# A static ring of five weight tiles, a separate tile of sums in the first FFN parts, and one more seven-product pair in groups 3 and 7

## The chip, the cores and the metric

The kernel runs on one core of one Trainium2 chip. TensorE does the matrix products, ScalarE and VectorE prepare the weights, GpSimd issues some of the DMAs and SyncE issues most of the rest. The metric is the device time of one execution in microseconds; the median of three runs of the kernel before is 2088.28 us (2087.98 to 2088.78).

## The reference

Two pre-norm layers work on a residual stream of 256 tokens by 2048 columns, all in float32. Layer 0 mixes tokens with two groups of heads (windowed attention and a chunked mLSTM), layer 1 with a forgetting attention. After the mixer each layer has the same feed-forward network, and only that is touched here:

```
x = x + mixer(rms_norm(x, g1))
y = rms_norm(x, g2)
x = x + (silu(y @ w_gate) * (y @ w_up)) @ w_down     # w_gate, w_up: 2048 x 5632, w_down: 5632 x 2048
```

A final norm ends it. The weights arrive in float32 and are read once.

## The kernel before

**Precision.** Each weight chunk is 128 partitions by 2 by 512 (256 rows of the matrix by 512 columns, 512 KB). ScalarE casts it to a shorter type (`hi`, a "cast"), VectorE subtracts that from the raw chunk (`lo`), and TensorE forms one product from three matmuls, hi by high part of the activations, lo by high part, hi by low part (`three`, L533 to L535). The function `split_chunk` (L188, L189) does this for a chunk as loaded, `split_plain` (L357, L358) for anything that was computed first. `hi` and `lo` rotate through eight pairs of tiles (`slot`).

**Staging of the feed-forward network.** The 5632 hidden columns are cut into 11 groups of 512 gate and 512 up columns, numbered 0 to 10. They are worked in three parts: groups 0 to 2, 3 to 6 and 7 to 10. Each part is followed by its share of the down-projection (two calls of `pair_group`, four blocks of 512 output columns). `ffn` holds these loops. The activations of a group are joined after its products: VectorE and ScalarE make silu(gate) times up in a tile `c`, four transposing DMAs on SyncE's queue (L709) turn it, and ScalarE and VectorE copy and split it into `mh` and `ml` during the next group. The last group of the first part uses TensorE transposes instead (L693).

**Pairs.** Inside a group (`pair_group`), eight pairs of 256 rows of the inner dimension are worked in the order of a table of (kind, pair). Kind 0, a plain pair, takes the gate chunk and the up chunk as they are: 8 products, 24 matmuls. Kind 1, a mixed pair, combines gate and up chunk before the products in the manner of Winograd and Strassen and takes seven products, 21 matmuls. A mixed pair needs the raw tile `ra` (gate), the raw tile `rb` (up), and the sum and differences of them. `ORDER` has three mixed pairs (1, 3 and 5, each between plain ones); `HEAVY`, used in groups 4, 5, 8 and 9 (`DENSE`), has four, each followed by a plain one.

**Where the sum is made.** In groups 3 to 10 and their down-projections (`adding`) the gate chunk is read a second time by a DMA that GpSimd issues and that adds into half of `rb` (L600). It waits for the load of `rb`, and the cast of `rb` waits for it. In groups 0 to 2 and their down-projection VectorE makes the sum (L606). Then, in both cases: `rb` is split into `hu`, `lu` (a 1024-element cast and subtraction), VectorE makes `rb[:,1]` (L608, 512) and all of `ra` (L610, 1024) from it, and those are split into `hc`, `lc` (512) and `hd`, `ld` (1024).

**What sets the order.** The program is written in one sequence; the framework's scheduler then decides the order of each engine's instructions and places the waits. The raw tiles of mixed pairs come from a pool with five buffers (`RAWS`, tag "raw", `load_raw` L135): a new tile takes the buffer that was given up first. Raw tiles of plain pairs come from another pool of four buffers. Each engine and each DMA queue works strictly in its own order.

## Time and profile before

| what | value |
|---|---|
| median of the runs | 2088.28 us (2087.98 to 2088.78, n = 3) |
| the profiled execution | 2086.12 us, its span 2084.4 us |
| TensorE busy in the span | 2066.4 us (99%) |
| VectorE busy | 1804.5 us (87%) |
| ScalarE busy | 1383.7 us (66%) |
| layer 0: groups 0 to 2 | 322.4 to 453.0 us |
| layer 0: down-projection of the first part | 453.0 to 519.0 us |
| layer 0: groups 3, 4, 5, 6 | from 519.0, 560.5, 601.3, 642.1 to 683.6 us |
| layer 0: groups 7 to 10 | 766.5 to 931.1 us |
| layer 1: groups 0 to 2 and their down-projection | 1385.0 to 1511.2 and to 1579.2 us |
| layer 1: groups 3 to 6, 7 to 10 | 1579.2 to 1743.7, 1826.7 to 1991.3 us |

In a timeline row the columns are start, duration, engine, source line, operation, output<-inputs, shape and count; in brackets stands the idle time before it and what ended that. A row with x6 stands for six instructions of its kind in a row. In a windows row the columns are the stretch, its length, then busy time (count) of TensorE, its weight loads, VectorE, ScalarE and GpSimd, the granted TensorE clock, the share of the DMA engines and GB/s. In a row of the groups, count, busy time and mean duration in ns are followed by the idle time before and what ended it. SPq is SyncE's DMA queue.

### The profile page before, as it was taken

To read this page: it belongs to the slowest core of one execution; us is meant where nothing else is said; L and a number is where in the kernel's file an instruction comes from. 1 tells how busy PE (TensorE), PEld (TensorE's weight loads), DVE (VectorE), ACT (ScalarE), POOL (GpSimd) and SP (SyncE) were. 2 spreads that over 40 slices of the span, in tenths; PEclk is the share of its full clock that TensorE was granted. 3 is DMA by queue.
4 is the path that set the end of the run, shared out by engine and by line. 5 is a ranking of instruction groups with operands and counts; after the bars stand their busy time and mean duration, and the time that the engine had idled before them with its cause. 6 is when DMAs were issued, how large, how long until landed. Compare 5 with 4: busy or idle time off the path is not lost.

```text
span 2084.4 us, 26995 instructions
## 1 busy us (share of the span) xinstructions
PE 2066.4 (99%) x9449; PEld 1713.1 (82%) x9449; DVE 1804.5 (87%) x2235; ACT 1383.7 (66%) x1760; POOL 113.2 (5%) x143
## 2 busy tenths in 40 slices
PE   9999999999999999999999999999999999999998
PEld 7878887887888888888888888888878888888887
DVE  6788768999899998998899688679998999899994
ACT  6777677765567656767677776687655677557763
POOL 1010000000000000000010000000000000000000
PEclk9999999999999999999999999999999999999999
DMA  8566577666778777778676766587657777867864
GB/s 292 175 208 197 189 252 227 187 204 213 210 225 265 232 233 237 226 240 218 205 211 208 229 198 185 155 265 227 222 174 235 236 220 239 259 205 209 265 206 150
DMA packets 320664, 455.07 MB, mean 218 GB/s; under 512 B 107644, under 2 KB 115856, under 8 KB 320400
## 3 DMA queue, kind: packets, MB, share of 16 engines
q1 hardware_dynamic: 307088, 426.27, 64.9%
q0 software_dynamic: 12720, 25.99, 6.8%
q8 instruction: 74, 1.21, 0.2%
q10 hardware_dynamic: 720, 1.09, 0.2%
q14 instruction: 62, 0.51, 0.1%
HBM read 428.87 MB, written 2.12 MB: 207 GB/s over the span
## 4 chain that ended last, share of the span: by engine, by line
PE 86%; DMA 4%; DVE 4%; ACT 4%; issue 3%; SPq 0%; ACTq 0%; POOLq 0%; POOL 0%; DVEq 0%
PE acc L533 19%; PE acc L534 19%; PE acc L535 19%; PE prod L533 5%; PE prod L534 5%; PE prod L535 5%; PE acc L224 4%; PE acc L223 4%; PE acc L225 4%; DVE lo L189 1%; DMA raw<-in_w_down_dram 1%; ACT hi L188 1%; DMA raw<-in_w_gate_dram 1%; PE p L387 1%; ACT box L323 1%
## 5 line engine op out<-in xcount | busy, mean ns | idle before, releaser
L189 DVE TENSOR_TENSOR lo<-raw,hi 128x1024 fp32r<-128x1024 f32 (+3 forms) x648 | 762.7, 1192 | 148.5 <-ACT hi L188 146.2
L188 ACT CAST hi<-raw 128x1024 fp32r<-128x1024 f32 (+3 forms) x648 | 654.0, 1027 | 352.9 <-PE acc L535 130.1
L534 PE MATMUL acc<-lo,xh 128*128 128x512 f32 x1272 | 495.0, 390 | 0.0
L535 PE MATMUL acc<-hi,xl 128*128 128x512 f32 x1272 | 493.9, 390 | 0.0
L533 PE MATMUL acc<-hi,xh 128*128 128x512 f32 x1272 | 480.5, 391 | 2.4 <-ACT hi L188 2.4
L357 ACT CAST hi<-raw 128x1024 fp32r<-128x1024 f32 (+1 forms) x323 | 286.9, 894 | 193.7 <-DVE raw L608 78.2
L358 DVE TENSOR_TENSOR lo<-raw,hi 128x1024 fp32r<-128x1024 f32 (+1 forms) x323 | 328.3, 1026 | 31.2 <-ACT hi L357 30.4
L533 PEld LDWEIGHTS acc<-hi,xh 128*128 128x128 f32 x1272 | 239.4, 188 | 53.6 <-ACT hi L188 4.0
L534 PEld LDWEIGHTS acc<-lo,xh 128*128 128x128 f32 x1272 | 239.6, 188 | 49.7 <-issue 0.2
L535 PEld LDWEIGHTS acc<-hi,xl 128*128 128x128 f32 x1272 | 239.3, 188 | 49.9
L534 PE MATMUL acc<-lo,mh 128*128 128x512 f32 x466 | 181.4, 390 | 0.0
L535 PE MATMUL acc<-hi,ml 128*128 128x512 f32 x466 | 180.8, 389 | 0.0
L533 PE MATMUL acc<-hi,mh 128*128 128x512 f32 x466 | 176.3, 389 | 4.4 <-ACT hi L357 4.4
L610 DVE TENSOR_TENSOR raw<-raw 128x1024 f32<-128x1024 f32 x103 | 125.6, 1220 | 0.9
L224 PE MATMUL acc<-lo,mh 128*128 128x512 f32 (+1 forms) x322 | 126.3, 392 | 0.0
L223 PE MATMUL acc<-hi,mh 128*128 128x512 f32 (+1 forms) x322 | 125.8, 391 | 0.0
L225 PE MATMUL acc<-hi,ml 128*128 128x512 f32 (+1 forms) x322 | 123.7, 391 | 0.0
L533 PEld LDWEIGHTS acc<-hi,mh 128*128 128x128 f32 x466 | 87.5, 188 | 23.0 <-ACT hi L357 4.9
L534 PEld LDWEIGHTS acc<-lo,mh 128*128 128x128 f32 x466 | 87.6, 188 | 18.2
L535 PEld LDWEIGHTS acc<-hi,ml 128*128 128x128 f32 x466 | 87.6, 188 | 18.2
L224 PE MATMUL acc<-lo,xh 128*128 128x512 f32 (+3 forms) x288 | 99.9, 347 | 0.2 <-DVE lo L189 0.2
L225 PE MATMUL acc<-hi,xl 128*128 128x512 f32 (+3 forms) x288 | 98.8, 344 | 0.0
(362 smaller groups left out, 3033.1 us busy)
## 6 DMA issues: line engine op xcount, KB each, us to landing
raw<-in_w_gate_dram SPq DMA_DIRECT2D x176, 512.0 KB, 5.3
raw<-in_w_up_dram SPq DMA_DIRECT2D x176, 512.0 KB, 5.2
raw<-in_w_down_dram SPq DMA_DIRECT2D x176, 512.0 KB, 5.7
raw<-in_w_in_odd_dram SPq DMA_DIRECT2D x88, 512.0 KB, 5.1
raw<-in_w_in_even_dram SPq DMA_DIRECT2D x51, 512.0 KB, 4.7
raw<-in_w_out_even_dram SPq DMA_DIRECT2D x32, 512.0 KB, 5.1
raw<-in_w_out_odd_dram SPq DMA_DIRECT2D x32, 512.0 KB, 4.7
raw<-in_w_gate_dram POOLq DMA_DIRECT2D x56, 256.0 KB, 5.7
```

Of the source, the lines that this page charges most:

```text
L188: latest[0] = nc.scalar.copy(hi[:, k, 0:n], raw[:, k, 0:n])
L189: nc.vector.tensor_tensor(out=lo[:, k, 0:n], in0=raw[:, k, 0:n], in1=hi[:, k, 0:n].bitcast(F32), op=ALU.subtract)
L223: nc.tensor.matmul(o, ah[:, ts], hi, start=(k == 0), stop=False)
L224: nc.tensor.matmul(o, ah[:, ts], lo, start=False, stop=False)
L225: nc.tensor.matmul(o, al[:, ts], hi, start=False, stop=(k == k_all - 1 and cs.stop == n))
L323: nc.scalar.copy(ju[:, :, b], turned[:, b, :, :, :].rearrange("p k t q -> p (k t q)"))
L357: nc.scalar.copy(dst_h, src)
L358: nc.vector.tensor_tensor(out=dst_l, in0=src, in1=dst_h.bitcast(F32), op=ALU.subtract)
L533: nc.tensor.matmul(o, ah, hi, start=start, stop=False)
L534: nc.tensor.matmul(o, ah, lo, start=False, stop=False)
L535: nc.tensor.matmul(o, al, hi, start=False, stop=stop)
L610: nc.vector.tensor_tensor(out=ra, in0=ra, in1=both, op=ALU.subtract)
```

## The change

There are three edits.

1. **Five fixed tiles.** The pool tag with five buffers is replaced by a list `ring` of five tiles, raw0 to raw4, made once per layer. In groups 3 to 10 and their down-projections `load_raw` takes them strictly in turn (ra, rb, ra, rb, ...), so the tile of an `rb` is the one that the `ra` of two mixed pairs earlier had, and the tile of an `ra` is the one that the `rb` of three pairs earlier had.
2. **Groups 0 to 2 and their down-projection.** Only raw0 to raw3 take loads there, and raw4 is a tile of sums, `t4`. The half `rb[:,1]` is split as loaded (512). VectorE then makes `t4[0]` = rb0 + ra0, `t4[1]` = rb1 - rb0, `ra[0]` = t4[0] - rb1, `ra[1]` = ra1 - ra0, four instructions of 512, and splits `t4` and `ra` (1024 each). The same seven products follow.
3. **Groups 3 and 7** use the table `PLAIN_FIRST`: four mixed pairs in the order 0, 1, 2, 3, 5, 4, 7, 6, where 1, 3, 5 and 7 are mixed; 3 and 5 are next to each other. The fourth pair's sums are already there, for `HEAVY`.

```diff
--- before.py
+++ after.py
@@ -35,6 +35,7 @@
 FILL = 16
 ORDER = ((0, 0), (1, 1), (0, 2), (1, 3), (0, 4), (1, 5), (0, 6), (0, 7))
 HEAVY = ((1, 1), (0, 0), (1, 3), (0, 2), (1, 5), (0, 4), (1, 7), (0, 6))
+PLAIN_FIRST = ((0, 0), (1, 1), (0, 2), (1, 3), (1, 5), (0, 4), (1, 7), (0, 6))
 FOURTH = 7
 DENSE = (4, 5, 8, 9)
 ADDING = 3
@@ -53,7 +54,6 @@
 W_RAWS = 4
 LATER = (6, 10, 3, 5)
 LATER_DOWN = (5, 6)
-RAWS = 5
 P_JOIN = 4
 COLD = 9
 TURNED = (0,)
@@ -125,6 +125,7 @@
     xt = gp.tile([P, KT, S], F32, name="xt")
 
     loaded = [None]
+    ring = []
 
     def load_raw(w, k0, c0, n, pool=wr, bufs=4, raws=None):
         if raws:
@@ -349,7 +350,7 @@
         elif n == 3:
             halves = [fp.tile([P, 3, NB], F32, tag=f"sd{i}", name="box", bufs=1)[:, 0:CK, :] for i in range(2)]
         else:
-            halves = [fp.tile([P, CK, NB], F32, tag="raw", name="box", bufs=RAWS) for _ in range(2)]
+            halves = ring[2:4]
         flat, turned = (a.rearrange("p a n -> p (a n)") for a in halves)
         return flat, turned.bitcast(U16).rearrange("p (b k t q) -> p b k t q", b=2, t=NT, q=P)
 
@@ -594,16 +595,14 @@
             first, last = 1 not in kinds[:pos], 1 not in kinds[pos + 1 :]
             if first:
                 prods = [bank(1 - par, "prod") for _ in range(4)]
-            ra, rb = (load_raw(w, k0, c0, NB, fp, W_RAWS if halves else RAWS, raws) for w, c0 in mats)
+            ra, rb = (load_raw(w, k0, c0, NB, fp, W_RAWS, raws) for w, c0 in mats)
             if adding:
                 (w, c0), part = mats[0], slice(k0 * P, (k0 + 1) * P)
                 nc.gpsimd.dma_start(rb[:, 0, :], w[part, c0 : c0 + NB], accum_op=ALU.add)
             hg, lg = split_chunk(ra, NB)
             run_due(todo, pos)
             hu, lu = slot()
-            if halves is None:
-                if not adding:
-                    nc.vector.tensor_tensor(out=rb[:, 0, :], in0=ra[:, 0, :], in1=rb[:, 0, :], op=ALU.add)
+            if adding:
                 split_plain(hu, lu, rb)
                 nc.vector.tensor_tensor(out=rb[:, 1, :], in0=rb[:, 0, :], in1=rb[:, 1, :], op=ALU.subtract)
                 both = rb[:, 1, :].rearrange("p (a n) -> p a n", a=1).broadcast_to([P, CK, NB])
@@ -614,6 +613,20 @@
                 split_plain(hd, ld, ra)
                 ht = [hu[:, 0, :], hd[:, 0, :], hc, hd[:, 1, :]]
                 lt = [lu[:, 0, :], ld[:, 0, :], lc, ld[:, 1, :]]
+            elif halves is None:
+                t4 = ring[4]
+                split_plain(hu[:, 1, :], lu[:, 1, :], rb[:, 1, :])
+                nc.vector.tensor_tensor(out=t4[:, 0, :], in0=rb[:, 0, :], in1=ra[:, 0, :], op=ALU.add)
+                nc.vector.tensor_tensor(out=t4[:, 1, :], in0=rb[:, 1, :], in1=rb[:, 0, :], op=ALU.subtract)
+                nc.vector.tensor_tensor(out=ra[:, 0, :], in0=t4[:, 0, :], in1=rb[:, 1, :], op=ALU.subtract)
+                nc.vector.tensor_tensor(out=ra[:, 1, :], in0=ra[:, 1, :], in1=ra[:, 0, :], op=ALU.subtract)
+                parts = []
+                for src in (t4, ra):
+                    hs, ls = slot()
+                    split_plain(hs, ls, src)
+                    parts.append((hs, ls))
+                ht = [parts[a][0][:, b, :] for a in range(2) for b in range(2)]
+                lt = [parts[a][1][:, b, :] for a in range(2) for b in range(2)]
             else:
                 split_plain(hu[:, 1, :], lu[:, 1, :], rb[:, 1, :])
                 nc.vector.tensor_tensor(out=ra[:, 0, :], in0=rb[:, 0, :], in1=ra[:, 0, :], op=ALU.add)
@@ -645,6 +658,7 @@
 
     def ffn(layer, fp, sx, x4, sd, key, todo, idx_next=None, key_next=None, finish=None):
         r = rstd(key)
+        early_ring = ring[0:4]
 
         def sums_x(pair):
             if pair == FOURTH:
@@ -664,8 +678,9 @@
                     x_of,
                     sums_x,
                     [(w_gate[layer], g * NB), (w_up[layer], g * NB)],
-                    HEAVY if g in DENSE else ORDER,
+                    HEAVY if g in DENSE else PLAIN_FIRST if g in (3, 7) else ORDER,
                     todo,
+                    raws=ring if g0 >= ADDING else early_ring,
                     adding=g0 >= ADDING,
                 )
                 todo = []
@@ -757,7 +772,8 @@
                         close(acc, n)
                     continue
                 plain, c = pair_group(
-                    fp, 1 - n0 // 2, m_of, sums_d, [(wd, n0 * NB), (wd, (n0 + 1) * NB)], order, todo, adding=g0 >= ADDING
+                    fp, 1 - n0 // 2, m_of, sums_d, [(wd, n0 * NB), (wd, (n0 + 1) * NB)], order, todo,
+                    raws=ring if g0 >= ADDING else early_ring, adding=g0 >= ADDING
                 )
                 todo = []
                 if end and idx_next is None:
@@ -777,12 +793,14 @@
             nd = max(len(mixed_of(o)) for o in DOWN.values())
             sx = [fp.tile([P, nx, 4, P], F32R, name=f"sx{i}", bufs=1) for i in range(2)]
             x4 = fp.tile([P, 2, P], F32R, name="x4", bufs=1)
+            ring.extend(fp.tile([P, CK, NB], F32, name=f"raw{i}", bufs=1) for i in range(5))
             todo = out_proj(w_out, idx, key, (*sx, x4, fp))
             sd = [fp.tile([P, nd, 4, P], F32R, tag=f"sd{i}", name=f"sd{i}", bufs=1) for i in range(2)]
             more = [[fp.tile([P, CK, NB], F32R, name=f"{a}{i}", bufs=1) for a in ("hi", "lo")] for i in range(2)]
             stock.extend(more + [slot() for _ in range(6)])
             ffn(layer, fp, sx, x4, sd, key, todo, **rest)
             stock.clear()
+            ring.clear()
 
 
     acc0 = new_acc()
```

The scheduler orders the changed program anew. Three places in which the order is different:

VectorE, early in group 3 of layer 0, from the last subtraction of the first mixed pair to the first of the third. Before, where the first pair has raw_4554, the second raw_4622 and raw_4624, the third raw_4690 (raw_4606, raw_4658 and raw_4674 are chunks of plain pairs):

```order
L358 TENSOR_TENSOR lo_3109<-raw_4554,hi_3108 128x1024
L371 TENSOR_TENSOR h_2402<-acc_4298,h_2402 128x512
L189 TENSOR_TENSOR lo1_3097<-raw_4606,hi1_3096 128x1024
L189 TENSOR_TENSOR lo_3099<-raw_4622,hi_3098 128x1024
L358 TENSOR_TENSOR lo_3101<-raw_4624,hi_3100 128x1024
L608 TENSOR_TENSOR raw_4624<-raw_4624 128x512
L610 TENSOR_TENSOR raw_4622<-raw_4622,raw_4624 128x1024
L358 TENSOR_TENSOR lo_3103<-raw_4624,hi_3102 128x512
L189 TENSOR_TENSOR lo_3107<-raw_4658,hi_3106 128x1024
L358 TENSOR_TENSOR lo_3105<-raw_4622,hi_3104 128x1024
L189 TENSOR_TENSOR lo_3109<-raw_4674,hi_3108 128x1024
L189 TENSOR_TENSOR lo0_3095<-raw_4690,hi0_3094 128x1024
```

And now, where the first pair has raw0 and raw1, the second raw2 and raw3, the third raw4 and raw0:

```order
L359 TENSOR_TENSOR lo_3112<-raw0_2413,hi_3111 128x1024
L359 TENSOR_TENSOR lo_3104<-raw3_2416,hi_3103 128x1024
L607 TENSOR_TENSOR raw3_2416<-raw3_2416 128x512
L609 TENSOR_TENSOR raw2_2415<-raw2_2415,raw3_2416 128x1024
L359 TENSOR_TENSOR lo_3106<-raw3_2416,hi_3105 128x512
L190 TENSOR_TENSOR lo_3110<-raw4_2417,hi_3109 128x1024
L359 TENSOR_TENSOR lo_3108<-raw2_2415,hi_3107 128x1024
L359 TENSOR_TENSOR lo_3112<-raw0_2413,hi_3111 128x1024
```

The first row gives raw0 up, and the last row needs raw0 loaded and added to again; six rows stand between, and the two subtractions of the plain pair that stood there have moved behind the third mixed pair.

SyncE's queue in group 5 of layer 0, around the four transposes of group 4's `c`. Before, in which raw_5335 and raw_5337 are the tiles of a mixed pair:

```order
L135 DMA raw_5269<-in_w_up_dram 128x2x512
L135 DMA raw_5303<-in_w_gate_dram 128x2x512
L135 DMA raw_5335<-in_w_gate_dram 128x2x512
L135 DMA raw_5319<-in_w_up_dram 128x2x512
L135 DMA raw_5337<-in_w_up_dram 128x2x512
L709 DMA_TRANSPOSE turned_5115<-c_5102 128x4x128 x2
L709 DMA_TRANSPOSE turned_5116<-c_5102 128x4x128 x2
L135 DMA raw_5382<-in_w_gate_dram 128x2x512
```

And now, in which raw2 and raw3 are the tiles of that pair:

```order
L136 DMA raw2_2415<-in_w_gate_dram 128x2x512
L136 DMA raw_5291<-in_w_up_dram 128x2x512
L136 DMA raw1_2414<-in_w_up_dram 128x2x512
L136 DMA raw4_2417<-in_w_gate_dram 128x2x512
L724 DMA_TRANSPOSE turned_5093<-c_5080 128x4x128 x2
L724 DMA_TRANSPOSE turned_5094<-c_5080 128x4x128 x2
L136 DMA raw3_2416<-in_w_up_dram 128x2x512
L136 DMA raw_5352<-in_w_gate_dram 128x2x512
```

The load of the pair's up chunk stood ahead of the transposes and stands behind them now.

ScalarE in group 0 of layer 0, around the last cast of the third mixed pair. Before, in which that is the cast of raw_3311:

```order
L357 CAST hi0_3094<-raw_3313 128x512
L188 CAST hi_3100<-raw_3385 128x1024
L188 CAST hi_3102<-raw_3401 128x1024
L188 CAST hi_3106<-raw_3458 128x1024
L357 CAST hi1_3096<-raw_3311 128x1024
L357 CAST xh_58<-s4_3330 128x3x128
L188 CAST hi_3108<-raw_3474 128x1024
```

And now, in which it is the cast of raw0:

```order
L189 CAST hi_3103<-raw_3385 128x1024
L189 CAST hi_3105<-raw_3401 128x1024
L358 CAST hi1_3099<-raw0_2413 128x1024
L189 CAST hi_3107<-raw_3417 128x1024
L557 COPY c_3433<-prod_3154 128x512
L189 CAST hi_3109<-raw_3458 128x1024
L189 CAST hi_3111<-raw_3474 128x1024
```

It stood behind the cast of raw_3458, a gate chunk of the next group, and stands four places ahead of it now.

## The prediction

> **What bounds the kernel now.** I read the page first: busy time, then the chain of waits.
>
> ```profile
> span 2084.4 us, 26995 instructions
> PE 2066.4 (99%) x9449; PEld 1713.1 (82%) x9449; DVE 1804.5 (87%) x2235; ACT 1383.7 (66%) x1760; POOL 113.2 (5%) x143
> PE 86%; DMA 4%; DVE 4%; ACT 4%; issue 3%; SPq 0%; ACTq 0%; POOLq 0%; POOL 0%; DVEq 0%
> ```
>
> TensorE sets the time, and VectorE is close behind it. So a matmul that is left out is worth its own time, and VectorE work is worth nothing until VectorE's lead over TensorE is used up. Next I cut the span into stages, as windows of layer 0: the down-projection of the first part, then groups 3, 4, 5 and 6.
>
> ```profile
> 453.00:519.00 66.00, 63.96 (x285) 52.61 (x284) 62.25 (x68) 34.74 (x40) 1.81 (x2) 1.00 0.63 200
> 519.00:560.50 41.50, 41.50 (x185) 34.36 (x184) 37.58 (x40) 23.23 (x26) 3.44 (x4) 1.00 0.79 231
> 560.50:601.30 40.80, 40.80 (x182) 33.78 (x181) 36.49 (x43) 28.37 (x32) 2.59 (x3) 1.00 0.74 211
> 601.30:642.10 40.80, 40.80 (x182) 33.78 (x181) 39.40 (x46) 28.64 (x33) 3.46 (x4) 1.00 0.84 258
> 642.10:683.60 41.50, 41.50 (x185) 34.37 (x184) 40.14 (x47) 28.81 (x32) 2.61 (x3) 1.00 0.84 243
> ```
>
> Groups 3 to 6 have no gap on TensorE: 41.50 of 41.50 us. There VectorE is idle for 3.92 us in group 3, 4.31 in group 4, and only 1.40 and 1.36 in groups 5 and 6. The first part does have gaps, and TensorE's timeline shows them, layer 0 first, then layer 1.
>
> ```profile
> 352.06 0.39 PE L534 MATMUL acc<-lo,xh 128*128 128x512 f32 x1
> 352.29 0.39 PE L535 MATMUL acc<-hi,xl 128*128 128x512 f32 x1
> 354.04 0.50 PE L534 MATMUL prod<-lo,sx 128*128 128x512 f32 x1 [0.68 <-DVE lo L358]
> 356.49 0.80 PE L533 MATMUL acc<-hi,xh 128*128 128x512 f32 x1 [1.72 <-ACT hi L188]
> 357.94 0.63 PE L534 MATMUL acc<-lo,xh 128*128 128x512 f32 x1
> 358.36 0.63 PE L535 MATMUL acc<-hi,xl 128*128 128x512 f32 x1
> 362.63 0.40 PE L534 MATMUL acc<-lo,xh 128*128 128x512 f32 x1
> 473.11 0.49 PE L533 MATMUL acc<-hi,mh 128*128 128x512 f32 x1 [2.04 <-ACT hi L357]
> 1417.68 0.50 PE L533 MATMUL acc<-hi,xh 128*128 128x512 f32 x1 [0.64 <-ACT hi L188]
> 1531.68 0.49 PE L533 MATMUL acc<-hi,mh 128*128 128x512 f32 x1 [2.39 <-ACT hi L357]
> 1533.75 0.63 PE L535 MATMUL prod<-hi,sd 128*128 128x512 f32 x1
> 1536.31 0.63 PE L534 MATMUL acc<-lo,mh 128*128 128x512 f32 x1
> ```
>
> The first two rows give TensorE's pace, 0.23 us from start to start (352.06 to 352.29; over long stretches 0.2267, which is 41.50 us by the 183 matmuls of group 3). The duration of 0.39 is latency. A wait of 0.68 us and one of 1.72 us follow; as a matmul's 0.39 ends about 0.16 after the next could start, they cost 0.84 and 1.88. Then the matmuls come 0.42 apart (357.94, 358.36), from 356.49 to 362.63 some fourteen of them at 0.20 extra, 2.8 us. That stall is 5.5 us. In the same way 473.11 costs 2.2, 1417.68 0.8, and 1531.68 2.6 plus 1.4 for the seven matmuls from 1533.75 to 1536.31 at the slow pace: in all 5.5 + 2.2 + 0.8 + 4.0 = 12.5. I call it 14 with the small waits around them.
>
> **The change, step by step.**
>
> *Fewer matmuls.* In groups 3 and 7 of both layers one plain pair (24 matmuls) becomes a mixed one (21). That is 4 x 3 = 12 matmuls by 0.2267 us: −2.7 us, if nothing waits.
>
> *The first part.* Before, a mixed pair there had these operations between its loads and its last split:
>
> ```profile
> L606 DVE TENSOR_TENSOR raw<-raw 128x512 f32<-128x512 f32 x26 | 17.9, 688 | 4.6 <-issue 2.3 <-DMA raw<-in_w_down_dram 0.9 <-DMA raw<-in_w_up_dram 0.8
> L608 DVE TENSOR_TENSOR raw<-raw 128x512 f32<-128x512 f32 x103 | 70.7, 686 | 0.9
> L610 DVE TENSOR_TENSOR raw<-raw 128x1024 f32<-128x1024 f32 x103 | 125.6, 1220 | 0.9
> L358 DVE TENSOR_TENSOR lo<-raw,hi 128x512 fp32r<-128x512 f32 x117 | 80.2, 685 | 8.3 <-ACT hi L357 8.3
> ```
>
> Now one 1024-element operation (1.220) becomes two of 512 (2 x 0.686): +0.15 us a pair, 26 pairs, +4.0 us of VectorE, hidden as long as VectorE has a lead; in the window 453 to 519 it is idle for 3.75 of 66 us. ScalarE has the same elements to cast. What counts is where things stand. The stall at 354 to 356 belongs to group 0's last mixed pair and the next group's first chunk. ScalarE's rows there:
>
> ```profile
> 355.40 1.04 ACT L188 CAST hi<-raw 128x1024 fp32r<-128x1024 f32 x1 [3.27 <-DMA raw<-in_w_gate_dram]
> 356.35 1.04 ACT L357 CAST hi<-raw 128x1024 fp32r<-128x1024 f32 x1
> ```
>
> ScalarE waits 3.27 us for a gate chunk, and the last cast of the mixed pair (356.35) is queued behind that wait. In the changed order it stands four places ahead of it, so TensorE can do that pair's last products (6 matmuls, 1.4 us) while the load lands. At 473.11 and 1531.68 TensorE waits for the cast of a whole `rb`, which needed VectorE's sum; now the half it needs there is cast as loaded, one wait fewer. Against that, raw4 as the single tile of sums makes each pair's sums wait for the last split of the pair before, and loads have four tiles, not five. The bounds are 0 (the gaps only move) and −14 (all gone). The rows are nearer to a half: the first stall loses some 1.4 of 2.7 us and perhaps its slow matmuls, the two others shorten. I take −7.
>
> *The ring in groups 3 to 10.* This is the term that decides. Follow one tile in groups 4 and 5, on VectorE, SyncE's queue, GpSimd and ScalarE:
>
> ```profile
> 591.57 0.69 DVE L358 TENSOR_TENSOR lo<-raw,hi 128x512 fp32r<-128x512 f32 x1
> 592.28 0.37 SPq L135 DMA_DIRECT2D raw<-in_w_up_dram  x1
> 597.75 0.86 POOL L600 DMA_DIRECT2D raw<-in_w_gate_dram  x1 [10.90 <-DVE raw L610]
> 602.19 1.05 ACT L357 CAST hi<-raw 128x1024 fp32r<-128x1024 f32 x1
> 612.77 2.96 DVE L358 TENSOR_TENSOR lo<-raw,hi 128x512 fp32r<-128x512 f32 x3
> 613.48 0.37 SPq L135 DMA_DIRECT2D raw<-in_w_up_dram  x1
> 614.39 6.28 SPq L709 DMA_TRANSPOSE turned<-c  x4
> 617.87 0.86 POOL L600 DMA_DIRECT2D raw<-in_w_gate_dram  x1 [13.08 <-DVE lo L189]
> 622.47 1.05 ACT L357 CAST hi<-raw 128x1024 fp32r<-128x1024 f32 x1 [1.88 <-DMA raw<-in_w_gate_dram]
> ```
>
> A 512-element `lo` ends at 592.26 and gives an `rb` up. SyncE loads the next up chunk into it at 592.28, GpSimd adds at 597.75, the cast runs at 602.19: 9.9 us. Two mixed pairs later it is the same: 613.45, 613.48, 617.87, and the cast at 622.47 came when the DMA did (idle 1.88 <-DMA). So this loop, up load, add, cast, use, up load, is on time without slack already: 20.28 us from cast to cast, and TensorE needs 20.40 for two mixed and two plain pairs (90 matmuls by 0.2267).
>
> In the ring an `rb` gets the tile of the `ra` of two mixed pairs earlier, and that one's last `lo` comes later than the `rb`'s. In the row 612.77 (three subtractions, the 512 first) the `ra` is done at 615.73, 2.28 us after 613.45. The loop is then: cast to last `lo` of `ra` 13.54 (602.19 to 615.73) and `lo` to cast 9.9, together 23.4 us against 20.40. By this each pair two places on comes 3.0 us later. From the second mixed pair of group 3 (where the ring is first full) to the last of group 5 there are five such steps: 15 us, less VectorE's lead over TensorE, for which I take the 3.9 us that it is idle in group 3: 11 us in a stretch of four groups. That is the one end. The other end: of the 13.54 us VectorE works partly for other pairs. The pair's own share is a cast (1.05), `lo` (1.22), L608 (0.69), L610 (1.22), `lo` of 512 (0.69), a plain `lo` (1.22) and the last (1.22), 7.3 us; with 9.9 that is 17.2, inside 20.40, and the ring costs 0. VectorE's order is fixed, though, and two places speak for the slower half. In group 5 the up load of the last mixed pair now stands behind the transposes, whose row lasts from 614.39 to 620.67, where before it went ahead of them at 613.48. In group 3 the raw0 of the first pair is loaded for the third, and only six VectorE instructions, 4 x 1.22 + 2 x 0.69 = 6.3 us, stand between its release and its next use, which is 9.9 away: 3.6 us and a cast idle on VectorE, while its work in that group rises by 4 x 1.22 + 2 x 0.69 − 2 x 1.22 = 3.8 us, all of its 3.92 of idle time. I take the middle, +6 us a stretch. There are four stretches (groups 3 to 6 and 7 to 10, twice): +24, with 0 and +44 as ends. Nothing has to be added for ScalarE, idle for 12 us or more in each of these groups, and GpSimd's four added DMAs are 0.86 us each on an engine that is busy 5%.
>
> *What a new wait brings along.* If a stall of 2 us in the adding groups is followed by slow matmuls as at 357, it costs up to 2.8 more; one in each stretch would be 11. I count none, since after the 2.04 us at 473.11 the granted clock of the whole window is still 1.00. [...]
>
> *The sum.* Against the profiled execution, 2086.1: −2.7 −7 +24 = 2100.4. The median of the runs is 2.2 us above the profiled execution, so 2102.6.
>
> **The rivals.**
>
> *Faster: the ring's delay is covered.* VectorE, waiting, has nothing else to do, so its share of the loop shrinks until the loop is 20.4 again; that is decided at a share of 10.5 us, between 7.3 and 13.5. Then the stretches cost 0 and 2102.6 − 24 = 2078.6 remains. For it speak the idle times of groups 3 and 4 (3.92 and 4.31), against it groups 5 and 6 (1.40, 1.36), too little to catch up.
>
> *No difference.* The stretches cost 2.4 us each and eat what the first part and the 12 matmuls bring: 2086.1 − 9.7 + 9.7 + 2.2, about 2088.
>
> *Much slower.* The loop keeps its 23.4 us, 11 us a stretch: 2078.6 + 44 = 2122.6.
>
> *The first part stays as it is.* Its gaps are set by the loads (the 3.27 us are a wait for a DMA), with four tiles no less than with five; the 7 us don't come: 2109.6.
>
> **How the numbers follow.** Forecast 0.33, much slower 0.14, first part unchanged 0.13; faster 0.28, no difference 0.12. A difference of 0.2%, 4 us, is about what this kernel's measurement can tell from none. So faster 0.28, same 0.12, slower 0.60. The range runs from a little below the covered ring (2078.6, and up to 4 more if the first part loses 11 instead of 7) to the loop at its full length: 2075 to 2122. The slower cases alone span 2094 to 2122.
>
> **What would show it.** Fewer matmuls: group 3 lasts 40.8 us, not 41.5, if nothing waits. The first part: no wait at the end of group 0, and the first down-projection near 64 us, not 66. The ring: in groups 4 and 5 the cast of `rb` has an idle time "<-DMA raw" of 2 to 3 us before it, SyncE's up load follows the last 1024 `lo` instead of the 512 one, and TensorE's busy time falls below the length of its windows in groups 4 to 6 and 8 to 10. I am wrong if those windows stay full: then the term of 24 is what failed.

## The result, and the profile after

| kernel | median (lowest to highest) | runs |
|---|---|---|
| before | 2088.31 us (2087.98 to 2088.78) | 4 |
| the change | 2173.64 us (2168.08 to 2175.34) | 4 |

The ratio is 1.0404, 95% interval 1.0385 to 1.0423: 85 us slower, where I had forecast 14. The page of the changed kernel has the same parts as before:

```profile
span 2172.6 us, 26985 instructions
PE 2101.5 (97%) x9437; PEld 1715.6 (79%) x9437; DVE 1820.8 (84%) x2277; ACT 1389.3 (64%) x1768; POOL 113.0 (5%) x147
PE 56%; DMA 15%; DVE 14%; issue 7%; ACT 7%; SPq 1%; ACTq 0%; POOL 0%; POOLq 0%; DVEq 0%
L358 ACT CAST hi<-raw 128x1024 fp32r<-128x1024 f32 (+1 forms) x335 | 295.5, 893 | 284.6 <-DMA raw<-in_w_gate_dram 103.5
```

TensorE holds 56% of the chain that ended last, before it was 86%, and DMA 15% where it was 4%. The casts of computed chunks (L358 of the changed kernel) now wait first of all for a DMA of gate weights; as loads of gate chunks are cast at L189, this is the adding DMA. TensorE's own waits, as the view of waits lists them (total, times, longest):

```profile
PE prod L534 <- ACT hi L358: 29.9, 22, 3.7
PE acc L534 <- ACT hi L358: 12.3, 5, 4.7
PE prod L535 <- DVE lo L359: 6.8, 11, 0.9
PE acc L534 <- ACT hi L189: 5.8, 10, 1.4
```

The windows show where it happens: groups 0 to 2 and their down-projection in layer 0, then the four stretches of four groups.

```profile
321.84:447.98 126.14, 124.98 (x550) 102.94 (x549) 120.35 (x159) 96.49 (x118) 0.69 (x1) 1.00 0.70 219
447.98:512.22 64.24, 64.24 (x285) 52.39 (x284) 60.16 (x69) 33.34 (x37) 1.81 (x2) 1.00 0.66 199
512.22:699.59 187.37, 172.50 (x725) 137.07 (x723) 155.44 (x174) 109.43 (x121) 12.96 (x15) 0.97 0.71 207
782.55:970.03 187.48, 173.96 (x725) 137.09 (x723) 159.52 (x179) 110.44 (x122) 12.96 (x15) 0.97 0.72 209
1621.59:1805.46 183.87, 173.01 (x725) 137.01 (x723) 155.85 (x174) 109.65 (x121) 12.79 (x15) 0.97 0.71 212
1888.42:2079.10 190.68, 175.56 (x725) 138.46 (x723) 159.55 (x179) 110.65 (x122) 12.81 (x15) 0.96 0.72 205
```

| stage | before, us | after, us | difference |
|---|---|---|---|
| groups 0 to 2, both layers | 256.7 | 252.3 | −4.4 |
| their down-projections | 134.0 | 128.5 | −5.5 |
| the four stretches (groups 3 to 6, 7 to 10) | 658.2 | 749.4 | +91.2 |
| last down-projection of layer 0 | 84.4 | 90.7 | +6.2 |
| all else | | | +0.7 |
| span | 2084.4 | 2172.6 | +88.2 |

A stretch without a wait would last 163.9 us (723 matmuls by 0.2267), so each of the four lost 20 to 27 us. Cut by groups, the first stretch loses most of it in groups 4 and 5, which had lasted 40.8 us each:

```profile
553.02:603.56 50.54, 44.52 (x181) 34.28 (x180) 41.63 (x48) 29.48 (x34) 3.09 (x4) 0.97 0.65 191
603.56:655.97 52.41, 45.01 (x182) 34.85 (x180) 42.16 (x48) 31.12 (x34) 3.44 (x4) 0.93 0.69 206
```

In the four stretches the first group (3 or 7) loses 0 to 2.6 us, the second 5.4 to 13.2, the third 7.8 to 12.7 and the last 1.2 to 3.8. Where groups 3 to 6 are named below for all four stretches, 7 to 10 are meant with them. The chain of waits inside layer 0's groups 4 and 5 shows what TensorE waits for (start, duration, what):

```profile
579.26 1.14 DVE lo L359
580.42 10.35 DMA raw<-in_w_up_dram
590.84 0.55 issue
591.39 5.62 DMA raw<-in_w_gate_dram
597.03 1.05 ACT hi L358
598.11 0.50 DVE lo L359
598.65 0.74 PE prod L534
599.39 0.43 PE acc L535
...
601.99 0.69 DVE c L559
```

This is the ring as the prediction described it: the last 1024-element `lo` of a gate tile ends at 580.40 and gives the tile up (the release), the up load starts at once, the add follows, the cast, and TensorE. What the prediction did not have is its length: 16.6 us from release to cast, where I had put 9.9.

### The profile page after: what moved, and what is told of

The parts are those of the page before. It is cut to its first block, busy times and chain, and to the rows that moved or that the text cites. A ratio compares the mean times of both kernels' runs of the same rounds, so it can differ in the third digit from the quotient of the medians.

```text
span 2172.6 us, 26985 instructions
## 1 busy us (share of the span) xinstructions
PE 2101.5 (97%) x9437; PEld 1715.6 (79%) x9437; DVE 1820.8 (84%) x2277; ACT 1389.3 (64%) x1768; POOL 113.0 (5%) x147
## 4 chain that ended last, share of the span: by engine, by line
PE 56%; DMA 15%; DVE 14%; issue 7%; ACT 7%; SPq 1%; ACTq 0%; POOL 0%; POOLq 0%; DVEq 0%
PE acc L534 12%; PE acc L535 11%; PE acc L536 11%; DMA raw<-in_w_gate_dram 6%; DMA raw<-in_w_up_dram 5%; DVE lo L190 4%; DVE lo L359 4%; PE acc L225 3%; PE acc L224 3%; PE acc L226 3%; PE prod L534 3%; PE prod L536 3%; PE prod L535 3%; DMA raw<-in_w_down_dram 2%; ACT hi L189 2%
## 5 line engine op out<-in xcount | busy, mean ns | idle before, releaser
L190 DVE TENSOR_TENSOR lo<-raw,hi 128x1024 fp32r<-128x1024 f32 (+2 forms) x644 | 758.1, 1192 | 151.8 <-ACT hi L189 146.3
L189 ACT CAST hi<-raw 128x1024 fp32r<-128x1024 f32 (+2 forms) x644 | 648.4, 1025 | 319.3 <-PE acc L536 134.8
L536 PE MATMUL acc<-hi,xl 128*128 128x512 f32 x1248 | 488.5, 394 | 0.0
L358 ACT CAST hi<-raw 128x1024 fp32r<-128x1024 f32 (+1 forms) x335 | 295.5, 893 | 284.6 <-DMA raw<-in_w_gate_dram 103.5
L359 DVE TENSOR_TENSOR lo<-raw,hi 128x1024 fp32r<-128x1024 f32 (+1 forms) x335 | 340.1, 1027 | 105.7 <-ACT hi L358 105.6
L601 POOL DMA_DIRECT2D raw<-in_w_gate_dram x60 | 51.7, 861 | 991.9 <-DMA raw<-in_w_up_dram 404.2
L609 DVE TENSOR_TENSOR raw<-raw,raw 128x1024 f32<-128x1024 f32 x81 | 98.8, 1220 | 0.8
```

The costliest lines, as they stand in the source:

```text
L189: latest[0] = nc.scalar.copy(hi[:, k, 0:n], raw[:, k, 0:n])
L190: nc.vector.tensor_tensor(out=lo[:, k, 0:n], in0=raw[:, k, 0:n], in1=hi[:, k, 0:n].bitcast(F32), op=ALU.subtract)
L358: nc.scalar.copy(dst_h, src)
L359: nc.vector.tensor_tensor(out=dst_l, in0=src, in1=dst_h.bitcast(F32), op=ALU.subtract)
L536: nc.tensor.matmul(o, al, hi, start=False, stop=stop)
L601: nc.gpsimd.dma_start(rb[:, 0, :], w[part, c0 : c0 + NB], accum_op=ALU.add)
```

## The experiments

Each kernel was timed against the kernel before on the same chip; the differences below are between the two medians of one such comparison. The framework orders a changed program anew, so that stages which no edit touches also move by up to 2 or 3 us.

### The parts of the change, one at a time

**The first part's edit alone**, with raw tiles from the pool and the old table in groups 3 to 10. These are the main lines of the edit; the same choice of the pool stands in the down-projections:

```diff
-            ring.extend(fp.tile([P, CK, NB], F32, name=f"raw{i}", bufs=1) for i in range(5))
+        ring.extend(fp.tile([P, CK, NB], F32, tag="raw", name="raw", bufs=RAWS) for _ in range(5))
-                    HEAVY if g in DENSE else PLAIN_FIRST if g in (3, 7) else ORDER,
+                    HEAVY if g in DENSE else ORDER,
-                    raws=ring if g0 >= ADDING else early_ring,
+                    raws=None if g0 >= ADDING else early_ring,
```

> The first part's edit alone: groups 3 to 10 take their raw tiles from the pool of five again and have the old table. All theories: the first part and its down-projection are 10 us shorter in the two layers together, the rest is as before, 2076 to 2081. If it stays near 2088, the gain of the first part in the change came from somewhere else.

2075.79 us, −10.8 us, ratio 0.9949 (0.9935 to 0.9964): at the lower end of what was expected, and faster than both kernels. The windows of groups 0 to 2 of layer 0, and of one stretch:

```profile
322.14:446.58 124.44, 124.44 (x550) 103.04 (x549) 118.45 (x157) 95.24 (x116) 0.69 (x1) 1.00 0.69 218
511.64:676.20 164.56, 164.56 (x727) 136.26 (x726) 153.68 (x173) 109.81 (x120) 12.09 (x14) 1.00 0.80 235
```

124.44 us is 549 matmuls at full pace: no gap is left there. The extra VectorE work (118.45 us in this window, 116.23 before) is hidden.

**The ring without the table**: the change with `ORDER` in groups 3 and 7.

```diff
-                    HEAVY if g in DENSE else PLAIN_FIRST if g in (3, 7) else ORDER,
+                    HEAVY if g in DENSE else ORDER,
```

> The change with the old table in groups 3 and 7, so ring and first part alone. Theory ring: groups 4 to 6 and 8 to 10 keep most of their stalls, 12 to 20 us a stretch, 2125 to 2165. Theory table: the stretches are full again and the first part's 10 us are a gain, about 2078.

2112.57 us, +26.0 us, ratio 1.0125 (1.0100 to 1.0150). Against the first part alone the ring costs 36.8 us. That is nearer to theory ring, though not in its range: the stretches last 170.0 to 172.8 us, only 5 to 8 more than before, and 12 us more are in the down-projections, which use the ring too.

**The table without the ring**: the kernel before with `PLAIN_FIRST` in groups 3 and 7.

```diff
-                    HEAVY if g in DENSE else ORDER,
+                    HEAVY if g in DENSE else PLAIN_FIRST if g in (3, 7) else ORDER,
```

> The kernel before with only the new table PLAIN_FIRST in groups 3 and 7 (raw tiles from the pool, first part as before). Theory ring (an up tile that waits for the last subtraction of a gate tile makes the loop of up load, add and cast too long): the table alone costs little; -2.7 us of matmuls against a few us of stalls, 2084 to 2096. Theory table (four mixed pairs, two of them next to each other, use up the lead of VectorE): the four stretches are each some 20 us longer here too, 2150 to 2175.

2106.41 us, +19.9 us, ratio 1.0097 (1.0076 to 1.0118): between the two expectations. The table costs something of its own, but its stretches are 168 to 171 us long, not 187.

**Two rings**: the change with gate tiles from three of the five and up tiles from the other two.

```diff
-                    raws=ring if g0 >= ADDING else early_ring,
+                    raws=(ring[0:3], ring[3:5]) if g0 >= ADDING else early_ring,
```

> The change with two rings in groups 3 to 10 in place of one: gate tiles take raw0 to raw2 in turn, up tiles raw3 and raw4, so an up load waits for the up tile of two pairs earlier, which is free 2.3 us sooner. Theory ring: the stalls shrink from 20 to 27 us a stretch to under 8, 2080 to 2105. Theory table: no great difference, over 2150. Theory queue (what counts is that up loads stand behind the transposes): in between, 2110 to 2145.

2093.32 us, +6.8 us, ratio 1.0031 (1.0020 to 1.0041). Its first stretch:

```profile
510.82:679.54 168.72, 165.57 (x724) 135.31 (x723) 157.70 (x178) 110.78 (x122) 12.95 (x15) 1.00 0.81 235
```

Theory ring holds: with static tiles too, 79 us go when an up load no longer waits for a gate tile. What is left over the first part alone, 17.5 us, is the table's own cost, 19.9 us in the run before this one.

So ring alone +37, table alone +18 to +20, and both together +96 (85.3 + 10.8): 40 us more than the two apart.

### Why ring and table together are so dear

**No adjacent mixed pairs**: the change with `HEAVY` in groups 3 and 7, four mixed pairs each followed by a plain one.

```diff
-                    HEAVY if g in DENSE else PLAIN_FIRST if g in (3, 7) else ORDER,
+                    HEAVY if g in (3, 4, 5, 7, 8, 9) else ORDER,
```

> The change with HEAVY in place of PLAIN_FIRST, so one ring of five and four mixed pairs a group, none adjacent. If the adjacent pairs are what makes ring and table together so dear: near 2115, the ring alone. If it is that the loop runs without slack from group 3 on: 2140 to 2180.

2171.28 us, +84.0 us, ratio 1.0405 (1.0379 to 1.0431), no different from the change. Adjacency is not the cause.

**No add**: the change without the adding DMA.

```diff
-                nc.gpsimd.dma_start(rb[:, 0, :], w[part, c0 : c0 + NB], accum_op=ALU.add)
```

> The change without the second, adding DMA of the gate chunk in groups 3 to 10 and their down-projections, so the sum of gate and up chunk is left out there and the up tile is ready some 6.5 us sooner; all else is the change. Theory loop (release of the gate tile, up load, add, cast, use, longer together than the 20.4 us of TensorE): without the add it is shorter than that, and the stretches are nearly full, 2070 to 2090. Theory VectorE (the stalls come from its added work and from its waits for TensorE): the stalls stay, over 2140.

2078.72 us, −8.5 us, ratio 0.9960 (0.9945 to 0.9974). Its first stretch:

```profile
513.25:678.13 164.88, 164.18 (x725) 135.62 (x723) 157.43 (x177) 110.91 (x122) 0.00 (x0) 1.00 0.68 217
```

With some 6 us less in the loop (0.6 until the add is issued, 5.3 for the add itself in the change) the ring and the table cost next to nothing, while VectorE does the same work (157.43 us) and the tiles go round the same ring. This decides for the loop of release, load, add, cast and use.

**The gate tile free sooner**: in groups 3 to 10 the gate tile is split ahead of the up tile.

```diff
+                hd, ld = slot()
+                split_plain(hd, ld, ra)
                 hc, lc = (a[:, 0, :] for a in slot())
                 split_plain(hc, lc, rb[:, 1, :])
-                hd, ld = slot()
-                split_plain(hd, ld, ra)
```

> The change with the gate tile's last split ahead of the up tile's in groups 3 to 10, so that in the one ring the tile that an up load waits for is free some 1 us sooner and the other later. Theory release: each link of the loop is about 1 us shorter, about ten links bind in a stretch, so some 5 to 10 us less a stretch, 2130 to 2155. Theory queue: the up loads still stand behind the transposes, 2160 to 2180.

2177.51 us, +90.2 us, ratio 1.0428 (1.0410 to 1.0445): no gain. Theory release is missed, and the time lies where theory queue had put it. From the second mixed pair of group 3 to the last of group 5, two mixed pairs take 25.4 us in the mean from the cast of one `rb` to that of the second after it, in the change 25.3; and the release comes 12.2 us after the cast, in the change 11.9, so the edit did not bring it forward. The split that moved forward needs a free `hi`, `lo` pair, and ScalarE waits for TensorE there: in the change's timeline of ScalarE stands, in the same loop,

```profile
580.53 1.05 ACT L189 CAST hi<-raw 128x1024 fp32r<-128x1024 f32 x1 [3.35 <-PE acc L536]
588.09 1.05 ACT L358 CAST hi<-raw 128x1024 fp32r<-128x1024 f32 x1 [2.19 <-DMA raw<-in_w_gate_dram]
597.03 2.51 ACT L358 CAST hi<-raw 128x1024 fp32r<-128x1024 f32 x3 [5.00 <-DMA raw<-in_w_gate_dram]
```

That the wait for TensorE took up the gain is an argument from this row; no run took that wait away.

**The transposes.** SyncE's queue in the change, early in group 4:

```profile
557.62 1.50 SPq L136 DMA_DIRECT2D raw<-in_w_up_dram  x2
568.75 0.37 SPq L136 DMA_DIRECT2D raw<-in_w_gate_dram  x1
570.98 5.13 SPq L724 DMA_TRANSPOSE turned<-c  x4
576.21 0.53 SPq L136 DMA_DIRECT2D raw<-in_w_up_dram  x1
576.85 0.41 SPq L136 DMA_DIRECT2D raw<-in_w_gate_dram  x1
577.35 0.42 SPq L136 DMA_DIRECT2D raw<-in_w_up_dram  x1
577.87 0.96 SPq L136 DMA_DIRECT2D raw<-in_w_gate_dram  x2
579.28 1.50 SPq L136 DMA_DIRECT2D raw<-in_w_up_dram  x2
```

After 559.1 one load is issued in 17 us, and then seven in 4.6 us. The up load at 576.21 is late, since its tile had been free since 571.5, and the one at 580.42 (the second of the last row) is under way together with the others and takes 10.35 us, where an up load takes 5.2 in the median of the kernel before. Two kernels take the transposes out of this queue. One issues them from ScalarE's queue:

```diff
-                        nc.sync.dma_start_transpose(turned[b][:, :, t, :], flat[:, b, t, :])
+                        nc.scalar.dma_start_transpose(turned[b][:, :, t, :], flat[:, b, t, :])
```

> The change with the transposes of c issued by ScalarE's queue instead of SyncE's. Measured so far: the ring alone costs 37 us over the first part's edit, the table alone 18, both together 98. Theory queue (a late TensorE makes c late, the transposes hold SyncE's queue until c is there, and the up loads behind them come later still): most of what is beyond the two single costs goes, 2110 to 2140. Theory release (only the wait of an up tile for a gate tile counts): the loop stays as long, 2160 to 2175.

2214.92 us, +127.6 us, ratio 1.0609 (1.0572 to 1.0645): worse than either expectation, and so no test of the queue, since ScalarE stands in the loop too. Early in group 4 the four transposes hold it for 5.3 us (575.58 to 580.88), and the cast behind them waits 3.5. The other leaves the transposing DMAs of groups 3 to 9 out and joins `c` as it is (so the down-projection gets it unturned):

```diff
-                    for t in range(NT):
+                    for t in range(NT if g0 < ADDING else 0):
                         nc.sync.dma_start_transpose(turned[b][:, :, t, :], flat[:, b, t, :])
```

> The change (one ring, new table) with the transposing DMAs of groups 3 to 9 left out (c is joined as it was). If transposes that hold SyncE's queue, and the bursts of loads behind them, lengthen the loop: the part of the 98 us beyond the ring's and the table's own (some 43) goes, and the table's own with it, 2095 to 2130. If the loop binds without them: 2150 to 2175.

2157.44 us, +70.0 us, ratio 1.0335 (1.0314 to 1.0356): 15 us better than the change. In the profiled executions the four stretches gain more, 720 us in place of 749, and the down-projections behind them last 8 us longer. So the transposes are a part, and not the larger one. The loop binds without them: two mixed pairs take 22.6 us in the mean there, 11.4 of it from release to cast, where the change has 25.3 and 13.4.

**The last mixed pair earlier**: the change with the order 0, 1, 2, 3, 5, 7, 4, 6 in groups 3 and 7.

```diff
-PLAIN_FIRST = ((0, 0), (1, 1), (0, 2), (1, 3), (1, 5), (0, 4), (1, 7), (0, 6))
+PLAIN_FIRST = ((0, 0), (1, 1), (0, 2), (1, 3), (1, 5), (1, 7), (0, 4), (0, 6))
```

> The change, one ring of five, with the order 0, 1, 2, 3, 5, 7, 4, 6 in groups 3 and 7. If the late c is what makes ring and table together cost 61 us more than the ring alone: 2105 to 2135. If it is the loop without slack from group 3 on, whatever the end of the group: 2155 to 2180.

2154.41 us, +66.8 us, ratio 1.0327 (1.0292 to 1.0361): just under the range of a loop without slack, far from the other. Two mixed pairs take 24.3 us there. What makes it 18.5 us better than the change was not followed up.

**What follows.** I followed every up tile of the four stretches through the traces, from its cast to the cast two mixed pairs later. From the second mixed pair of group 3 to the last of group 5 there are five such steps. In the change a step takes 25.3 us in the mean (24.7 to 25.5 by stretch), 11.9 of it from the cast to the release and 13.4 from the release to the next cast. TensorE needs 20.4 for two mixed and two plain pairs. Five such steps lose 5 x 4.9 = 24 us, and the stretches lost 20 to 27.

The steps are not alike. The first, second and fourth take 18.3 to 24.9 us, the third and the fifth 30.3 to 33.9 in all four stretches. These two lie inside groups 4 and 5, where `c` of the group before is combined and turned. In them the release comes 13.3 to 17.4 us after the cast, and the up load is issued 2.9 to 6.1 us after the release, each time within 0.2 us of the end of the four transposes ahead of it on SyncE's queue.

With the ring and the old table group 4 loses nothing in any stretch. Groups 4 and 5 of its first stretch:

```profile
554.00:594.80 40.80, 40.80 (x181) 33.78 (x180) 36.90 (x44) 28.85 (x32) 3.48 (x4) 1.00 0.71 210
594.80:639.35 44.55, 42.25 (x181) 33.34 (x180) 38.09 (x44) 27.89 (x31) 2.59 (x3) 1.00 0.75 222
```

There group 3 has three mixed pairs in 41.5 us, 27.7 us for two, so the loop gains on TensorE: the adds for the second and third mixed pair of group 4 had landed 4.0 to 6.3 us before their casts, and in the change 0.1 to 3.6. So the table takes away the only groups in which the loop was shorter than the products. That this lead, and a `c` that is late because TensorE is late, make up the 40 us is an argument from these figures; how the 40 us divide was not tried. That the loop's length decides was tried, by taking the add away, and what the transposes add to it, by leaving them out.

### What the table costs by itself

With two rings and with the pool the table has one stall in each stretch, in group 5 or 9. TensorE's timeline in the kernel with two rings, first and second stretch:

```profile
605.34 0.39 PE L534 MATMUL prod<-hi,sx 128*128 128x512 f32 x1
608.21 0.50 PE L534 MATMUL prod<-hi,sx 128*128 128x512 f32 x1 [2.48 <-ACT hi L358]
609.15 0.49 PE L534 MATMUL prod<-hi,xh 128*128 128x512 f32 x1 [0.45 <-ACT hi L189]
609.49 0.39 PE L535 MATMUL prod<-lo,sx 128*128 128x512 f32 x1
609.72 0.40 PE L536 MATMUL prod<-hi,sx 128*128 128x512 f32 x1
...
859.27 0.49 PE L534 MATMUL prod<-hi,sx 128*128 128x512 f32 x1 [1.86 <-ACT hi L358]
860.22 0.80 PE L534 MATMUL prod<-hi,xh 128*128 128x512 f32 x1 [0.46 <-ACT hi L189]
860.81 0.63 PE L535 MATMUL prod<-lo,sx 128*128 128x512 f32 x1
861.24 0.63 PE L536 MATMUL prod<-hi,sx 128*128 128x512 f32 x1
```

Five kernels looked for its cause. Pool and `HEAVY` in groups 3 and 7, so no adjacent mixed pairs (the diffs of the pool and of `HEAVY` stand above):

> The first part's edit, raw tiles from the pool, and groups 3 and 7 with the table HEAVY, four mixed pairs each followed by a plain one. If the 18 us of the table alone come from the two adjacent mixed pairs: 2073 to 2076, the twelve matmuls as a gain. If they come from VectorE's added work, which leaves group 5's loop without lead: 2085 to 2100.

2092.21 us, +4.9 us, ratio 1.0025 (1.0014 to 1.0035). That is 15.6 us over the first part alone, where the table of the change cost 17.5 and 19.9, and the stall is there in every stretch. So adjacency is at most a small part here.

Two rings, and in groups 3 and 7 the 1024-element subtraction on the gate tile is left out:

```diff
-                nc.vector.tensor_tensor(out=ra, in0=ra, in1=both, op=ALU.subtract)
+                if not lean:
+                    nc.vector.tensor_tensor(out=ra, in0=ra, in1=both, op=ALU.subtract)
```

> The kernel with two rings and the new table (2093.3), with the 1024-element subtraction on the gate tile left out in groups 3 and 7, so VectorE has there 4 x 1.2 us less, about what the fourth mixed pair brings. If the 18 us of the table alone come from VectorE's added work in groups 3 and 7: 2073 to 2079. If they come from the up loads and adds that follow each other faster there: 2087 to 2094.

2092.54 us, +5.3 us, ratio 1.0027 (1.0017 to 1.0038): VectorE's added work is not it. Two rings, and in groups 3 and 7 the add is left out:

```diff
-                nc.gpsimd.dma_start(rb[:, 0, :], w[part, c0 : c0 + NB], accum_op=ALU.add)
+                if not lean:
+                    nc.gpsimd.dma_start(rb[:, 0, :], w[part, c0 : c0 + NB], accum_op=ALU.add)
```

> The kernel with two rings and the new table (2093.3), with the adding DMA left out in groups 3 and 7 alone (the sum is left out there), so that the up tiles are ready 6.5 us sooner in these two groups. If the table's 18 us come from VectorE's added work: no great change, 2087 to 2094. If they come from the loop of up load and add, whose slack group 3 uses up: 2073 to 2081.

2093.67 us, +6.5 us, ratio 1.0030 (1.0019 to 1.0040): nor are these groups' adds. In all three the stall stayed where it was. Pool, with the last mixed pair earlier, as above:

> The first part's edit, raw tiles from the pool, and in groups 3 and 7 four mixed pairs in the order 0, 1, 2, 3, 5, 7, 4, 6, so that the last mixed pair ends as early in the group as in the old table and two plain pairs follow it. If the table's 18 us come from c being joined late (its transposes started 12.9 us after the group's end with the new table and 5.7 with the old one, and held SyncE's queue until then): most of the 18 us go, 2073 to 2081. If the place of the last mixed pair does not matter: 2088 to 2096.

2109.16 us, +21.5 us, ratio 1.0108 (1.0093 to 1.0123): worse than either expectation. Groups 5 and 9 lose 6.5 to 7.3 us there, and the transposes still started 10 us after the end of group 3. That says nothing about the late `c`. Two rings, and the transposing DMAs of groups 3 and 7 left out (`c` is joined unturned there):

```diff
-                    for t in range(NT):
+                    for t in range(NT if g not in (3, 7) else 0):
                         nc.sync.dma_start_transpose(turned[b][:, :, t, :], flat[:, b, t, :])
```

> The kernel with two rings and the new table (2093.3) with the transposing DMAs of groups 3 and 7 left out (what is joined there is c as it was, not turned). In it these transposes started 5.7 us later than with the old table, held SyncE's queue, seven loads followed in 4 us, and the next up load with its add took 15 us. If that is where the table's own 18 us come from: 2073 to 2081. If not: 2088 to 2095.

2085.19 us, −2.2 us, ratio 0.9990 (0.9980 to 0.9999). Of the 17.5 us some 9 are gone, 6 of them in the four stretches. With the table, `c` of group 3 is ready later, since a mixed pair stands in the last place but one. SyncE's rows of its transposes, in the kernel with two rings and new table and then in the one with pool and old table, where group 3 ends at 551.6 and at 553.1:

```profile
564.54 5.27 SPq L724 DMA_TRANSPOSE turned<-c  x4
```

```profile
558.81 5.12 SPq L726 DMA_TRANSPOSE turned<-c  x4
```

They start 12.9 us after the group's end instead of 5.7, and the loads behind them come in a burst, seven in 4 us, with up loads of mixed pairs among them. Without these transposes about half of the table's cost is gone. The other half, stalls that still make 2 to 4 us a stretch and a few us in other stages, stays open.

## Why the prediction was wrong, point by point

**Fewer matmuls, −2.7 us: right**, and swallowed by the waits. 723 matmuls a stretch where there were 726, and group 3 lasts the 40.8 us that were named in two of the four stretches; without the add the stretches come to 164.9 to 166.2 us, near the 163.9 they would need.

**The first part, −7 us: right.** −9.9 us in the change, −10.8 us alone. The cast that stands ahead of the waiting one and the half that is cast as loaded did what was argued, and more: groups 0 to 2 run without a gap in both layers when the edit stands alone. How much each of the two brought was not tried. The single tile of sums cost these groups nothing.

**The ring, +6 us a stretch: the step that failed.** Place, order and direction of the mechanism were as told; its size was 20 to 27 us. Four things in this step were too kind.

- *The middle between two ends.* The lower end let VectorE's share of the loop shrink to the pair's own 7.3 us when it starves. It was 11.9 us in the mean of the five steps, 8.2 to 17.4 one by one, and over the 10.5 at which the loop would have been covered. VectorE's order is fixed, and between a cast and the release stand other pairs' subtractions and the combination of `c` (601.99 in the chain above), which waits for TensorE, which waits for the cast.
- *9.9 us from release to cast.* That was read from two places in which all went fast; the second, from 613.45 to 622.47, is 9.0, not "the same". The mean in the change is 13.4, the largest miss of the step: 1.8 until the load is issued, 4.6 for the load, 0.6 until the add is issued, 5.7 for the add and 0.6 until the cast. The medians of the kernel before would have given 5.2 for the load, 0.6 until the add is issued and 5.9 for the add, 11.7. The wait for SyncE's queue, up to 6.1 us in the long steps, had no term.
- *A lead of 3.9 us.* It was taken from group 3's idle VectorE time, though the same paragraph has the new table use that up. From the fourth mixed pair of a stretch to the last of its third group, the casts of `rb` came 2.6 to 3.3 us after the add had landed in the kernel before, and 0.5 to 0.6 after it in the change (means by stretch).
- *No slow matmuls.* I left the 11 us for them out, as a wait of 2.04 us had not brought any. In the four stretches of the change 72 matmuls start 0.43 after the one before instead of 0.23, some 14 us in all, as in TensorE's timeline after this wait:

```profile
598.65 0.74 PE L534 MATMUL prod<-hi,xh 128*128 128x512 f32 x1 [3.66 <-ACT hi L358]
599.19 0.63 PE L535 MATMUL acc<-lo,xh 128*128 128x512 f32 x1
599.61 0.63 PE L536 MATMUL acc<-hi,xl 128*128 128x512 f32 x1
```

With the upper end, the medians and no lead the same step gives 13.54 + 11.7 − 20.4 = 4.8 us a step, 24 a stretch, and the sum 2086.1 − 2.7 − 7 + 97 + 2.2 = 2175.6. The rows for it were on the table. That this sum meets the measured time is luck in part: 13.54 is 1.6 us more than the runs have in its place and 11.7 is 1.7 less, it takes all steps as alike, and the down-projections are not in it.

**The transposes** were named as speaking for the slow half and priced at nothing beyond it. Leaving them out is worth 15 us of the 85 (29 us in the four stretches of the profiled executions), and in the change they stand ahead of the up load in each of the long steps.

**The down-projections** after the adding groups were not looked at. They take tiles from the same ring: 6.2 us in the last one of layer 0 here.

**The rivals.** "Much slower" had the mechanism and 2122.6, which still had the fast 9.9 us and the lead in it. "Covered" is what the kernel without the add showed: 20.1 us for two mixed pairs.

## What to carry to other kernels

When a buffer's release, its load and its first use form a loop, compare the loop's length with what the busiest engine needs for one turn. Take medians for the transfers, and take the turn in which the loop's engines and queues have the most other work, not a quiet one: each turn that is too long is paid for, and no engine's idle share warned of it here. Ask what stands ahead of the load on its queue at the moment of the release. A static ring must give each tile's next use to the tile that is free first; here three tiles for gates and two for ups did as well as a pool, where one ring of five cost 79 us. A change that makes the busiest engine's work shorter in the only places where such a loop had slack can take away more than it gives: with the one ring, the twelve matmuls that the table saves are worth 2.7 us, and the table made the kernel 59 us longer.

## What the runs showed of the hardware

After its longest waits in the change TensorE went on at the slow pace, 0.43 us from start to start in place of 0.23. Each of the four waits over 3 us there (3.66 at 598.65, 4.70 at 614.07, 4.71 at 1719.47, 3.21 at 1951.34) was followed by 7 to 12 matmuls 0.43 apart, and one of 2.41 us by none:

```profile
845.63 0.50 PE L534 MATMUL prod<-hi,sx 128*128 128x512 f32 x1 [2.41 <-ACT hi L358]
845.97 0.39 PE L535 MATMUL prod<-lo,xh 128*128 128x512 f32 x1
```

Shorter ones went both ways. In the kernel with two rings a wait of 2.48 and 0.45 us (608.21, 609.15) was followed by matmuls 0.23 apart, and one of 1.86 and 0.46 us at the same place of the next stretch (859.27, 860.22) by six matmuls 0.43 apart. Why one short wait is followed by slow matmuls and another is not, these runs do not show.

Loads that were issued close together took longer to land: of the seven of the change issued between 576.21 and 580.8 the first took 4.10 us and the last 10.35, and two up loads of the kernel before with next to nothing beside them (issued at 1433.79 and 375.42) took 3.6 and 3.7. The 971 transfers of SyncE's queue landed in the order of their issue, in the kernel before and in the change.
